# A row gradient streamed through three slots: where the third store is issued, and how loads and stores take turns on one DMA queue

## The chip, the cores and the metric

The kernel runs on one core of one Trainium2 chip. The metric is the device time of one execution in microseconds (us); the time before is the median of three runs, 1417.23 us, with 1416.08 and 1429.57 as the lowest and the highest. Engines are named as in the profile: DVE (VectorE), POOL (GpSimd) and SP (SyncE, which only issues DMAs here); SPq and POOLq are their instruction queues.

## The reference

```python
def setup_inputs():
    return {"x": np.random.randn(8192, 8192).astype(np.float32)}

def reference(x):
    return np.gradient(x, axis=1)
```

Along each row of 8192 numbers the result is `(x[j+1] - x[j-1]) / 2` inside, `x[1] - x[0]` in the first column and `x[8191] - x[8190]` in the last. So 268.44 MB are read from HBM and 268.44 MB are written, with one subtraction and one halving for each element.

## The kernel before, in words

The 8192 rows are cut into `nsets` = 32 tiles of 256 rows. A tile puts two whole rows into each of the 128 partitions, 64 KB a partition and 8.39 MB in all; in HBM a tile is one contiguous block. Tile `i` lives in slot `i % 3` of three buffers (`slots`, line 41). A slot has 64 spare elements ahead of the data, and the result is written in place, shifted down by these 64 elements, so one slot holds a tile from the start of its load to the end of its store.

For each tile the work is:

- the load (line 61, in `load`), one DMA on SP's queue. It may start when the store of tile `i - 3`, the last user of the slot, has landed (line 62).
- `ends` (line 71), a small subtraction on POOL: the four end values of the two rows a partition holds, taken before they are overwritten. It is the first instruction that waits for the load.
- the difference (line 82), one DVE instruction over 16,382 elements a partition, which subtracts the neighbours, halves, and writes in place. It waits for `ends`.
- the copy of the end values into the first and last columns (line 93), on POOL where `i % 5` is 1 or 3, else on DVE.
- the store. For `i % 3` of 0 and 1 it is one DMA on SP's queue (line 103). For `i % 3` = 2 it is two DMAs on POOL's own queue (line 99), each of 64 partitions, with the rows in HBM grouped as 8 groups of 8.

The last tile is computed and stored in two halves (`nr`, line 78).

The order on each queue is the order in which the program is written (`manual_schedule`, line 64). Three loads come first; then, after the store of every tile with `i % 3` = 2, the next three loads are issued together (lines 108 to 110). So SP's queue holds load, load, load, store, store, and again load, load, load, store, store. SP issues one DMA after another, and an instruction that waits for a semaphore holds back all those behind it. The function `chain` (line 46) names the waits that each instruction needs.

Of the kernel before, what the change touches and what calls it, by code (L numbers as in the profile page):

```python
# [1 line left out]

# [4 lines left out]


@with_exitstack
def kernel(  # L10
    ctx: ExitStack,
    tc: tile.TileContext,
    x: bass.AP,
    out: bass.AP,
):

    nc = tc.nc
    P = nc.NUM_PARTITIONS
    n, m = x.shape
    R = 2  # L30
    NB = 3
    SH = 64
    W = R * m
    nsets = n // (P * R)
    f32 = x.dtype

    x_sets = x.rearrange("(s p t) m -> s p (t m)", p=P, t=R)
    out_sets = out.rearrange("(s p t) m -> s p (t m)", p=P, t=R)

    pool = ctx.enter_context(tc.tile_pool(name="pool", bufs=1))  # L40
    slots = [pool.tile([P, SH + W], f32, name=f"slot{k}", tag=f"slot{k}") for k in range(NB)]
    ends = pool.tile([P, nsets, R, 2], f32, name="ends", tag="ends")
    loads, stores = [], [[] for _ in range(nsets)]
    in_front = {}

    def chain(i, ins, *needed):

        group, engine = f"slot{i % NB}", ins.ins.engine  # L50
        keep = [o.ins for o in needed]
        if in_front.get(engine, (None,))[0] == group:
            keep.append(in_front[engine][1])
        tc.declare_no_dep(ins.ins, group=group, keep=keep, reason="implied by the needed step")
        tc.add_to_no_dep_group(group, ins.ins)
        in_front[engine] = group, ins.ins
        return ins

    def load(i):
        b = slots[i % NB]  # L60
        ins = nc.sync.dma_start(out=b[:, SH : SH + W], in_=x_sets[i])  # L61
        loads.append(chain(i, ins, *(stores[i - NB] if i >= NB else [])))

    with tc.manual_schedule():
        for i in range(NB):
            load(i)
        for i in range(nsets):
            b = slots[i % NB]
            xin = b[:, SH : SH + W].rearrange("p (t m) -> p t m", m=m)

            ins = nc.gpsimd.tensor_sub(  # L71
                out=ends[:, i, :, :],
                in0=xin[:, :, 1 : m : m - 2],
                in1=xin[:, :, 0 : m - 1 : m - 2],
            )
            at = [chain(i, ins, loads[i])]
            last = i == nsets - 1
            nr = 1 if last else R
            for r in range(0, R, nr):
                c0, c1 = r * m + 1, (r + nr) * m - 1  # L80

                ins = nc.vector._custom_dve(  # L82
                    dve_ops.TENSOR_TENSOR_REDUCE_SUB_MAX,
                    out=b[:, c0:c1],
                    in0=b[:, SH + c0 + 1 : SH + c1 + 1],
                    in1=b[:, SH + c0 - 1 : SH + c1 - 1],
                    s0=0.0,
                    s1=0.5,
                )
                halved = chain(i, ins, *at)  # L90
                res = b[:, r * m : (r + nr) * m].rearrange("p (t m) -> p t m", m=m)
                placer = nc.gpsimd if i % 5 in (1, 3) and not last else nc.vector
                ins = placer.tensor_copy(out=res[:, :, 0 : m : m - 1], in_=ends[:, i, r : r + nr, :])  # L93
                placed = chain(i, ins, halved)
                if i % NB == NB - 1:

                    for h in range(2):
                        rows = out_sets[i, 64 * h : 64 * h + 64, :].rearrange("(a c) w -> a c w", a=8)
                        ins = nc.gpsimd.dma_start(out=rows, in_=b[64 * h : 64 * h + 64, 0:W])  # L99
                        stores[i].append(chain(i, ins, placed))  # L100
                    at = [halved]
                    continue
                ins = nc.sync.dma_start(
                    out=out_sets[i, :, r * m : (r + nr) * m], in_=b[:, r * m : (r + nr) * m]
                )
                stores[i].append(chain(i, ins, placed))
                at = [halved]
            if i % NB == NB - 1:
                for k in range(i + 1, min(i + 1 + NB, nsets)):
                    load(k)  # L110


# [1 line left out]
_INS = ['x']  # L114
_OUTS = [((8192, 8192), 'float32')]


# [23 lines left out]
```

## Time and profile before

| | |
|---|---|
| median of three runs | 1417.23 us (1416.08 to 1429.57) |
| the profiled execution's own time | 1416.08 us |
| its span, first to last instruction | 1414.2 us |
| DVE busy | 554.8 us, 39% of the span, 54 instructions |
| the difference, line 82, full tile | 31 instructions of 17.2 us |
| POOL busy | 19.8 us, 1% of the span |
| POOL's 20 store issues, line 99 | 11.0 us in all, 0.55 us each |
| SP's load issues, line 61 | 32, 0.34 us each (median) |
| SP's store issues, line 103 | 23, 0.34 us each (median) |
| HBM | 268.44 MB read, 268.44 MB written, 380 GB/s over the span |

How to read the profile: times are in us unless marked ns. A group of instructions is named by its line, engine and operation, and by the tensors it writes and reads (`slot<-in_x_dram` is a load, `out_dram<-slot` a store). The page of the profile has the busy share of each engine in 40 equal slices of the span, and under it the mean busy share of the 16 DMA engines and the GB/s that they moved. The queue numbered q1 is the one that SP's DMAs go through, q0 the one of POOL's. A share of the 16 engines is the time that a queue's packets took, divided by 16 times the span; where one DMA engine has packets of two queues under way, both are counted, so that a sum can pass 1. In the table of stretches, "DMA share" is the same for a stretch of time, and the last column is GB/s.

### The profile page before, as it was taken

Reading aid. Unit: us, or ns where it says so; the run is one execution under the profiler, and the core shown is the slowest. Engines: PE = TensorE matmul, PEld = TensorE weight load, DVE = VectorE, ACT = ScalarE, POOL = GpSimd, SP = SyncE. Lnnn points to the kernel's source line nnn. Section 1 sums busy time; section 2 is a strip of 40 time slices with the busy share of each in tenths; the row PEclk is TensorE's granted clock in tenths of the full one; section 3 lists DMA queues with packets and bytes.
Section 4 is the critical chain, followed back from the end, with each engine's and each line's share of the span. In section 5 each row is a group of like instructions: output and inputs, shape, how many; then the busy total and the mean of one; then the engine's idle time right before and its main releaser. Section 6 shows DMA issues by size and latency. Waiting matters only on the chain.

```text
span 1414.2 us, 269 instructions
## 1 busy us (share of the span) xinstructions
DVE 554.8 (39%) x54; POOL 19.8 (1%) x68
## 2 busy tenths in 40 slices
DVE  3820481048006700860094028304900950283063
POOL 0000000000000000000000000000000000000000
DMA  9999999999999999999999999999999999999959
GB/s 415 415 356 285 436 432 319 324 437 430 319 358 430 434 297 393 426 393 323 397 408 345 361 424 397 326 382 412 443 326 400 432 369 356 417 402 360 380 235 391
DMA packets 9522, 536.89 MB, mean 380 GB/s; under 512 B 1200, under 2 KB 1200, under 8 KB 1200
## 3 DMA queue, kind: packets, MB, share of 16 engines
q1 hardware_dynamic: 7920, 452.99, 76.9%
q0 software_dynamic: 1600, 83.89, 20.5%
q14 instruction: 2, 0.02, 0.0%
HBM read 268.44 MB, written 268.44 MB: 380 GB/s over the span
## 4 chain that ended last, share of the span: by engine, by line
another core or an unknown queue 47%; DMA 33%; DVE 15%; issue 3%; POOL 1%; SPq 0%; POOLq 0%
DMA slot<-in_x_dram 18%; DVE slot L82 15%; DMA out_dram<-slot 14%; POOL out_dram L99 0%; POOL ends L71 0%; SPq L61 0%; DVE slot L93 0%; POOL slot L93 0%; POOLq L136 0%; POOLq L99 0%
## 5 line engine op out<-in xcount | busy, mean ns | idle before, releaser
L82 DVE CUSTOM_DVE_ANT_0 slot<-slot 128x16382 f32<-128x16382 f32 (+1 forms) x33 | 551.3, 16706 | 837.0 <-POOL ends L71 837.0
L71 POOL TENSOR_TENSOR ends<-slot 128x4 f32<-128x4 f32 x32 | 6.3, 196 | 1039.1 <-DMA slot<-in_x_dram 1039.1
L99 POOL DMA_DIRECT2D out_dram<-slot x20 | 11.0, 553 | 107.8 <-DVE slot L93 106.6
L93 POOL COPY slot<-ends 128x4 f32<-128x4 f32 x12 | 2.3, 190 | 207.9 <-DVE slot L82 207.9
L93 DVE COPY slot<-ends 128x4 f32<-128x4 f32 (+1 forms) x21 | 3.6, 172 | 0.7
L125 POOL MEMSET const-float32-0.0<- 128x1 f32 x1 | 0.1, 98 | 0.2 <-issue 0.2
L125 POOL MEMSET const-bfloat16-1.0<- 128x1 bf16 x1 | 0.1, 101 | 0.0
L125 POOL MEMSET const-uint8-127<- 128x1 uint8 x1 | 0.1, 101 | 0.0
L125 POOL MEMSET const-float32-1.0<- 128x1 f32 x1 | 0.1, 98 | 0.0
## 6 DMA issues: line engine op xcount, KB each, us to landing
out_dram<-slot SPq DMA_DIRECT2D x2, 4096.0 KB, 20.2
slot<-in_x_dram SPq DMA_DIRECT2D x32, 52.2
out_dram<-slot SPq DMA_DIRECT2D x21, 41.5
out_dram<-slot POOLq DMA_DIRECT2D x20, 49.5
```

Source lines behind the costliest of these rows:

```text
L71: ins = nc.gpsimd.tensor_sub(out=ends[:, i, :, :], in0=xin[:, :, 1 : m : m - 2], in1=xin[:, :, 0 : m - 1 : m - 2],)
L82: ins = nc.vector._custom_dve(dve_ops.TENSOR_TENSOR_REDUCE_SUB_MAX, out=b[:, c0:c1], in0=b[:, SH + c0 + 1 : SH + c1 + 1], in1=b[:, SH + c0 ...
L93: ins = placer.tensor_copy(out=res[:, :, 0 : m : m - 1], in_=ends[:, i, r : r + nr, :])
L99: ins = nc.gpsimd.dma_start(out=rows, in_=b[64 * h : 64 * h + 64, 0:W])
L125: nc = _bacc.Bacc("TRN2", target_bir_lowering=False, num_devices=1)
```

## The change

The store of every tile goes through SP's queue as one DMA; POOL issues no DMA any more. The loads follow in pairs: after the store of each odd tile `i` come the loads of tiles `i + 2` and `i + 3`, in place of three loads after every third tile. SP's queue then holds load, load, load, store, store, load, load, store, store, load, load, and so on. The number of slots, the tiles, the computation, and the engine that places the end values of each tile stay as they were; DVE keeps its instructions in their order; SP's list grows by the 10 stores and POOL's loses its 20 halves. Lines move up in the changed kernel: the load is line 59, `ends` line 69, the difference line 80, the copy line 91 and the store line 93.

```diff
@@
-    loads, stores = [], [[] for _ in range(nsets)]
+    loads, stores = [], [None] * nsets
@@ def load(i):
         ins = nc.sync.dma_start(out=b[:, SH : SH + W], in_=x_sets[i])
-        loads.append(chain(i, ins, *(stores[i - NB] if i >= NB else [])))
+        loads.append(chain(i, ins, *([stores[i - NB]] if i >= NB else [])))
@@
                 placed = chain(i, ins, halved)
-                if i % NB == NB - 1:
-
-                    for h in range(2):
-                        rows = out_sets[i, 64 * h : 64 * h + 64, :].rearrange("(a c) w -> a c w", a=8)
-                        ins = nc.gpsimd.dma_start(out=rows, in_=b[64 * h : 64 * h + 64, 0:W])
-                        stores[i].append(chain(i, ins, placed))
-                    at = [halved]
-                    continue
                 ins = nc.sync.dma_start(
                     out=out_sets[i, :, r * m : (r + nr) * m], in_=b[:, r * m : (r + nr) * m]
                 )
-                stores[i].append(chain(i, ins, placed))
+                stores[i] = chain(i, ins, placed)
                 at = [halved]
-            if i % NB == NB - 1:
-                for k in range(i + 1, min(i + 1 + NB, nsets)):
+            if i % 2 == 1:
+                for k in range(i + 2, min(i + 4, nsets)):
                     load(k)
```

## The prediction

> **What bounds the kernel now.** I read the page first, then SP's waits, a table of stretches cut at POOL's stores, the timeline of one group of three tiles, and the start of the chain.
>
> ```profile
> span 1414.2 us, 269 instructions
> ...
> DVE  3820481048006700860094028304900950283063
> ...
> DMA  9999999999999999999999999999999999999959
> GB/s 415 415 356 285 436 432 319 324 437 430 319 358 430 434 297 393 426 393 323 397 408 345 361 424 397 326 382 412 443 326 400 432 369 356 417 402 360 380 235 391
> ...
> q1 hardware_dynamic: 7920, 452.99, 76.9%
> q0 software_dynamic: 1600, 83.89, 20.5%
> ```
>
> The 16 DMA engines are busy from end to end; DVE is not (39%). So the DMA engines are the bound. But equal busy shares do not move equal data: a slice moves 415 to 443 GB/s, or 285 to 330. Per queue: q1 moves 452.99 MB in 76.9% of 1414.2 us, 416.5 GB/s; q0, which is POOL's, 83.89 MB in 20.5%, 289 GB/s. The next view cuts the time at POOL's stores: from their issue until the third load behind them is issued (odd rows), and from there to the next (even rows).
>
> ```profile
> 80.60:146.50 65.90, 0.00 (x0) 1.18 (x2) 1.00 1.02 318
> 146.50:217.20 70.70, 52.01 (x5) 0.78 (x4) 1.00 0.99 430
> 217.30:286.30 69.00, 0.00 (x0) 1.06 (x2) 1.00 1.00 319
> 286.30:357.20 70.90, 51.84 (x4) 0.97 (x5) 1.00 1.00 433
> ...
> 826.20:897.00 70.80, 52.02 (x5) 0.78 (x4) 1.00 0.94 408
> ```
>
> The last two columns are the DMA share and GB/s. With POOL's store under way the engines are as busy (1.00 to 1.02) and move 318 or 319 GB/s; without it, 430 or 433. The nine even stretches give 408 to 433, about 424 weighted by length. DVE works in the even rows only, so it is not DVE that slows the transfers.
>
> ```profile
> 178.37 19.64 SPq L103 DMA_DIRECT2D out_dram<-slot  x2
> 179.98 0.20 POOL L71 TENSOR_TENSOR ends<-slot 128x4 f32<-128x4 f32 x1 [1.64 <-DMA slot<-in_x_dram]
> ...
> 199.31 0.20 POOL L71 TENSOR_TENSOR ends<-slot 128x4 f32<-128x4 f32 x1 [19.14 <-DMA slot<-in_x_dram]
> ...
> 217.27 1.09 POOL L99 DMA_DIRECT2D out_dram<-slot  x2 [17.76 <-DVE slot L93]
> 218.60 67.73 SPq L61 DMA_DIRECT2D slot<-in_x_dram  x3
> ```
>
> This is the clock of the transfers. The second load of this group lands at 179.98 and the third at 199.31: 19.33 us for 8.39 MB, 434 GB/s. A store issued at 178.37 stands behind that load; the load that waits for it goes out at 218.60, 19.29 us after 199.31. So a store takes what a load does, and passing from loads to stores cost nothing here. Then the three loads take SP 67.73 us to issue, since each waits for a store and the third for both POOL halves.
>
> ```profile
> 0.74 21.93 DMA slot<-in_x_dram
> ```
>
> The first load, on an empty queue, takes 21.93 us from issue to landing. So 2.6 us (21.93 - 19.33) are start and landing together: a DMA issued 2.6 us or more before the one ahead of it lands leaves no gap.
>
> **The loss in time.** POOL's stores are issued at 80.55, 217.27, 357.22 and so on to 1284.73: 133.8 us from one to the next. A group is six transfers, 6 x 19.33 = 116.0. So 17.8 us a group are lost, 160.2 over nine groups. From 1286.04, when the last two loads go out, six transfers are left: 1286.04 + 116.0 + 1.0 (last landing to end of span) = 1403.0, against 1414.2: 11.2 more. Without these 171.4 us the span would be 1242.8. From the other side: 22.67 (first landing) + 63 x 19.33 + 1.0 = 1241.5. The two agree; I take 1242.
>
> **The change part by part.**
>
> *POOL's stores go to SP's queue* (20 DMAs out, 10 in). The ten tiles' transfers then cost 19.33 each as the others do, and the packets of two queues no longer meet on the engines. That is the whole gain, -171 to -173.
>
> *POOL loses 20 issues of 0.55 us,* 11.0 us in all: nothing, POOL is busy 1%. *SP gains 10 issues of 0.34 us,* 3.4 us: nothing while a transfer stands in the queue, 3.4 at most.
>
> *The order of SP's queue.* Here a wait could come in, because SP stops at each load. Let T = 19.33 and let the store of tile i-1 (i odd) start at 0. It lands at T, and the load of tile i+2, which waited for it, is issued; the queue still has the store of i, T of work against the 2.6 it needs: 16.7 to spare. The store of i lands at 2T, and the load of i+3 is issued, again with 16.7 to spare. Behind it SP was holding the store of i+1, long computed: issued at 2T, needed at 4T, no delay. The load of i+2 lands at 3T; `ends`, the difference and the copy take 17.7 (first tile: 22.74 to the store's issue at 40.43), so the store of i+2 is issued at 3T + 17.7 and needed at 5T: 38.7 - 17.7 - 2.6 = 18.4 to spare. The next load waits for the store of i+1, which lands at 5T. No link is late, for every pair; DVE needs 35 us of 77.3. The covers are the transfer ahead in the queue. If they were gone, each pair would pay up to 17.7 + 2.6 = 20.3.
>
> ```profile
> SPq L61 <- DMA out_dram<-slot: 809.0, 29, 54.0
> ```
>
> These waits remain, of about one T in place of up to 54.0, and stay hidden for the same reason. At the end the store of tile 30 no longer stands behind a late load, and the two halves of tile 31 (8.7 us of DVE each) are ready before the store of 30 is through: cost nothing.
>
> *From stores to loads, 15 times.* Before, a load behind a store on q1 always had POOL's store beside it, so the price of this passage is not shown clean. Lower end 0: loads to stores at 199.31 cost 0. Upper end by the largest excess of a transfer without POOL's: the third load lands at 62.58, 20.53 after the second at 42.05, 1.2 too much; 15 x 1.2 = 18. I take 0.3 each, near the rows without excess (the same pair of loads is 19.31 to 19.34 in the later groups I read): 5. A gain is excluded, as no transfer took less than 19.3.
>
> **Sum.** 1242 + 5 = 1247 of span; the profiled execution's own time is 1416.08 for 1414.2, so +1.9: **1249**. The median of the runs shown is 1.15 above the profiled one.
>
> [...]
>
> **The rivals.**
>
> *Not POOL's queue but the passage from stores to loads is what is slow (slower).* For: each slow stretch begins just where loads follow stores, and what is left when POOL's store is gone is not shown. Against: q1's packets move 416.5 GB/s by their own share and q0's 289, and the slow stretch lasts some 65 us, while a passage is a moment. Price: 17.8 each, 15 of them in place of ten groups: 1244 + 267 = 1511. It decides from (1416 - 1244) / 15 = 11.5 us a passage.
>
> *The queue runs dry part of the way (faster, less).* An engine that is ahead of the slowest by over 16.7 us has nothing to do until the landing is complete. For: near the end of before the engines are out of step; slices of one us there show one tenth busy:
>
> ```profile
> DMA  9999799999967313031130311311011109109090
> ```
>
> (1340 to 1380 us). Against: this follows POOL's stores, and the changed kernel has only one form of transfer, with equal shares. Price: 5 us a pair gives 1249 + 75 = 1324; 2 to 10 give 1279 to 1399.
>
> *No change.* The engines' busy share is already 97% and the bytes are the same; if mixing reads and writes set the 380 GB/s, the time stays 1416. Against: the even stretches hold loads and stores too.
>
> **How the numbers follow.** Forecast 0.74, with a range of its own of 1242 to 1272: below, no cost at the passages; above, all data at the 424 GB/s of the even stretches (536.89 MB / 424 = 1266, + 4.3 for start and end, + 1.9). Partly dry 0.12, no change 0.04, slower 0.10. All data at q1's 416.5 would give 1295; a range of 1240 to 1300 holds the forecast and the near half of the second case, 0.80. A change under 1% is about what a measurement here cannot tell from none: faster 0.86, same 0.04, slower 0.10.
>
> **What would show it.** Right: q0 gone from the table of queues, slices of 425 to 435 GB/s throughout, loads landing 19.3 apart in pairs and pairs 77.3 apart, one store wait of about 19 us before each load. Wrong: a low slice in each pair (passage), tenths under 9 in the DMA line (dry), or a load landing more than 20.5 after the one before with the queue full.

## The result, and the profile after

| | before | after |
|---|---|---|
| median of four runs each, us | 1419.72 (1416.08 to 1429.57) | 1248.37 (1248.06 to 1249.45) |
| ratio, with its 95% interval | | 0.8785 (0.8738 to 0.8832) |
| profiled execution, and its span, us | 1416.08, 1414.2 | 1248.15, 1246.1 |

The change takes 171 us off. The forecast was 1249 with a span of 1247. Here and below, medians and ranges are over all runs of a kernel, and ratios over its runs within 1.5% of the fastest, against runs of the kernel before that were taken with them. The page of the changed kernel, with the same lines as were shown of before:

```profile
span 1246.1 us, 240 instructions
...
DVE  2851905519055190551905519064290642806423
...
DMA  9999999999999999999999999999999999999998
GB/s 404 438 438 429 414 435 438 438 438 433 433 429 431 429 433 435 435 438 431 433 438 427 425 438 438 438 429 435 431 438 435 429 427 433 435 433 435 435 438 362
...
q1 hardware_dynamic: 9360, 536.88, 99.7%
```

The DMA line was nines in all slices but one before, and is again: it could not tell the two kernels apart. The GB/s line does. No slice between the first and the last is under 414, where before it fell every few slices, down to 285 and near the end to 235. The bound is the same, the 16 DMA engines (97.4% before, both queues together, and 99.7%); what they move is not (380 GB/s over the span before, 431 after).

The timeline of the changed kernel from the first pair on (`ends` at line 69 is the first to see a load land; line 59 are the loads, line 93 the stores):

```profile
81.73 20.05 SPq L59 DMA_DIRECT2D slot<-in_x_dram  x2
101.82 36.71 SPq L93 DMA_DIRECT2D out_dram<-slot  x2
120.45 0.20 POOL L69 TENSOR_TENSOR ends<-slot 128x4 f32<-128x4 f32 x1 [57.85 <-DMA slot<-in_x_dram]
...
140.00 0.20 POOL L69 TENSOR_TENSOR ends<-slot 128x4 f32<-128x4 f32 x1 [1.84 <-DMA slot<-in_x_dram]
...
159.38 19.82 SPq L59 DMA_DIRECT2D slot<-in_x_dram  x2
...
198.04 0.20 POOL L69 TENSOR_TENSOR ends<-slot 128x4 f32<-128x4 f32 x1 [57.84 <-DMA slot<-in_x_dram]
```

In this pair the loads land 19.55 apart, and the next pair follows 77.59 later (120.45 to 198.04); four transfers at 19.33 are 77.32. Over the whole span the pairs follow each other every 77.58 on average. The two stores behind a pair go out within 36.71 us, one at once and one when its tile is computed, well inside the 77. And SP's own waits:

```profile
SPq L59 <- DMA out_dram<-slot: 577.8, 29, 21.6
```

29 loads wait for a store, 577.8 us in all, 19.9 each; before it was 809.0, with one of 54.0. The waits have become even, not short, and they are hidden: a transfer always stands ahead in the queue, and no slice between the ends falls under 414 GB/s.

### The profile page after: what moved, and what is told of

The parts are those of the page before. It is cut to its first block, busy times and chain, and to the rows that moved or that the text cites. A ratio compares the mean times of both kernels' runs of the same rounds, so it can differ in the third digit from the quotient of the medians.

```text
span 1246.1 us, 240 instructions
## 1 busy us (share of the span) xinstructions
DVE 554.8 (45%) x54; POOL 8.9 (1%) x48
## 3 DMA queue, kind: packets, MB, share of 16 engines
q1 hardware_dynamic: 9360, 536.88, 99.7%
## 4 chain that ended last, share of the span: by engine, by line
DMA 52%; DVE 21%; another core or an unknown queue 20%; issue 5%; SPq 0%; POOL 0%; POOLq 0%
DMA slot<-in_x_dram 45%; DVE slot L80 21%; DMA out_dram<-slot 7%; SPq L93 0%; POOL ends L69 0%; DVE slot L91 0%; POOL slot L91 0%; POOLq L126 0%; SPq L59 0%
```

## The experiments

The sum had come out, but it rested on a reading that had not been tested: that POOL's store was slow because the packets of two queues met on the engines. That theory (the queue) stood against the form of the store (two halves of 64 partitions, grouped by 8), and both against the order of loads and stores (the passage). Each edit below is against the kernel before, unless it says otherwise. "Third store" is that of the tiles with `i % 3` = 2.

### Without the pairs: three and three on SP

This takes away POOL's queue and the halves together, as the change does, and keeps the order by threes.

```diff
-                if i % NB == NB - 1:
-                    for h in range(2):
...
-                    continue
                 ins = nc.sync.dma_start(
```

> Only the queue of the third store is changed: it goes through SP's queue as one DMA, and the order stays three loads, then three stores. The theory that the second queue or the form of its store was the loss (both call for it) expects 64 transfers of 19.33 us and 10 passages from stores to loads at the 0.25 us that the changed kernel shows a pair: 1245 to 1250. The rival that the order by pairs brings part of the gain expects a time above 1265, with low slices where three loads wait for three stores.

1248.03 us (1247.75 to 1248.18), ratio 0.8767 (0.8709 to 0.8825). The whole gain is there without the pairs. In the same place of the timeline three loads now go out in 39.33 us, where before they took 58.1 to 67.7:

```profile
81.61 39.33 SPq L61 DMA_DIRECT2D slot<-in_x_dram  x3
139.76 0.20 POOL L71 TENSOR_TENSOR ends<-slot 128x4 f32<-128x4 f32 x1 [77.24 <-DMA slot<-in_x_dram]
```

The order by pairs brings nothing of its own.

### The order alone: pairs, with POOL's halves kept

This is the changed kernel with the block of lines 95 to 102 of before put back.

```diff
+                if i % NB == NB - 1:
+                    for h in range(2):
...
+                    continue
                 ins = nc.sync.dma_start(
```

> Only the order is changed: loads by pairs as in the changed kernel, but every third store stays on POOL's queue in two halves. The theory that the loss belongs to POOL's store expects ten times some 17 us above 1248, so 1390 to 1430, and low slices of about 320 GB/s wherever q0 is at work. The rival that the order brings part of the gain expects 1250 to 1370.

1489.72 us (1483.76 to 1501.59), ratio 1.0451 (1.0362 to 1.0541): above both expectations, and slower than before. SP's waits and a stretch of it show why:

```profile
SPq L59 <- DMA out_dram<-slot: 979.7, 24, 101.7
```

```profile
240.00:297.00 57.00, 17.22 (x1) 0.38 (x2) 1.00 1.00 278
```

The queues in the last 17 us of that stretch, from 280 to 297 us:

```profile
q0 software_dynamic: 51, 3.15, 83.5%
q1 hardware_dynamic: 29, 0.85, 14.6%
```

A load that waits for a store stands at the head of SP's queue for up to 101.7 us (54.0 before), and a store that is ready stands behind it: one whose tile was done at 258.87 goes out at 301.93. At the end of that wait q1 has little to offer (14.6%), and the engines move POOL's slow store nearly alone: 4.00 MB of both queues in these 17 us, 235 GB/s. So POOL's halves are slow even where few packets of q1 run beside them. The pairs are harmless with all stores on the one queue and costly beside POOL's halves; pairs beside a whole store on POOL were not run.

### The form: POOL's store in one piece

```diff
-                    for h in range(2):
-                        rows = out_sets[i, 64 * h : 64 * h + 64, :].rearrange("(a c) w -> a c w", a=8)
-                        ins = nc.gpsimd.dma_start(out=rows, in_=b[64 * h : 64 * h + 64, 0:W])
-                        stores[i].append(chain(i, ins, placed))
+                    ins = nc.gpsimd.dma_start(out=out_sets[i], in_=b[:, 0:W])
+                    stores[i].append(chain(i, ins, placed))
```

> The kernel before, with POOL's store as one DMA of 128 partitions in place of two halves of 64 grouped by 8; it stays on POOL's queue. If two queues on the same engines are the cause (queue theory), the time stays at 1390 to 1430 and q0's packets remain slow. If the form of the store is the cause (form theory), the time falls to 1250 to 1270 with 425 to 435 GB/s while both queues are at work.

1266.2 us (1252.66 to 1285.33), ratio 0.8819 (0.8726 to 0.8912). The two fastest of the four runs took 1252.66 and 1258.11. With the second queue still in use, nearly all of the gain is there. From 80 to 125 us, while POOL's store and SP's loads run side by side:

```profile
DMA packets 352, 19.92 MB, mean 443 GB/s; under 512 B 48, under 2 KB 48, under 8 KB 48
...
q1 hardware_dynamic: 208, 11.53, 59.2%
q0 software_dynamic: 144, 8.39, 43.0%
```

A share divided by the megabytes is the price of a byte: 59.2 / 11.53 = 5.13 for q1 and 43.0 / 8.39 = 5.13 for q0. A byte costs the same on both, and together they move 443 GB/s. In the page of before the same division gives 76.9 / 452.99 = 0.170 and 20.5 / 83.89 = 0.244. It was not the queue that made q0's bytes dear. The queue theory falls as the main cause; what is left of it is the distance of this kernel from 1248, 4 to 10 us in the two fastest runs.

### The form without the second queue: the halves on SP

```diff
-                        ins = nc.gpsimd.dma_start(out=rows, in_=b[64 * h : 64 * h + 64, 0:W])
+                        ins = nc.sync.dma_start(out=rows, in_=b[64 * h : 64 * h + 64, 0:W])
```

> The kernel before, with the two halves of 64 partitions grouped by 8 issued on SP's queue in place of POOL's: the form without the second queue. Queue theory: 1245 to 1255. Form theory: each of the 20 halves uses only some of the 16 engines; if both halves fall on the same eight, each group has eight engines idle for up to 19.3 us, 1249 + 10 x 19.3 = 1442; if they spread over all, but with slow packets, 1350 to 1420.

1450.94 us (1433.69 to 1499.5, ten runs), ratio 1.0130 (1.0074 to 1.0187). The form alone carries all of the loss; the 1.3% beyond it are a small difference. Stretches of the first group in the profiled run, one of 1464.48 us: ahead of the halves, then in the first half:

```profile
85.00:95.00 10.00, 0.00 (x0) 0.00 (x0) 1.00 0.97 419
...
108.00:118.00 10.00, 0.00 (x0) 0.00 (x0) 1.00 1.03 210
```

The loads that wait for the last store ahead of the halves, and for the halves:

```profile
101.17 38.64 SPq L61 DMA_DIRECT2D slot<-in_x_dram  x2
```

All 16 engines are busy (a mean share of 1.03), at 210 GB/s, half of the 419. The first of the two loads goes out at 101.17, when the last store ahead of the halves has landed, and the second, whose issue of 0.33 ends that 38.64, at 139.5, when both halves have. So the third store takes some 38.3 us, twice 19.3. The expected 1442 is near the time, but it had eight engines idle, and by the share of 1.03 none is: the packets are slow on all. On POOL's queue the same halves cost 1.3% less in sum. That q1's transfers run beside them there is the likely reason; it was not tried by itself.

### Grouping, or halves?

Four edits took the form apart, all with the third store on SP's queue. In the first two it is one DMA of 128 partitions, its HBM rows grouped as 16 groups of 8, and as 8 groups of 16:

```diff
-                    for h in range(2):
-                        rows = out_sets[i, 64 * h : 64 * h + 64, :].rearrange("(a c) w -> a c w", a=8)
-                        ins = nc.gpsimd.dma_start(out=rows, in_=b[64 * h : 64 * h + 64, 0:W])
+                    rows = out_sets[i].rearrange("(a c) w -> a c w", a=16)
+                    ins = nc.sync.dma_start(out=rows, in_=b[:, 0:W])
```

> [...] The rival that the split into halves of 64 partitions, each on some of the engines, is the cause: 1246 to 1255.

1247.99 us (1247.1 to 1248.14), ratio 0.8770 (0.8714 to 0.8825). The grouping as the cause had been put at 1400 to 1470.

> [...]

1247.89 us in a single run, where the grouping as the cause had been put at up to 1441, or at 1550 to 1870. These ranges were the author's estimates; how the groups are shared out among the engines is in no trace. Both expectations built on the grouping fell: with all 128 partitions in the DMA, the grouping costs nothing, in either form (1248.03 without it, in three and three). The third has the halves without the grouping:

```diff
-                        rows = out_sets[i, 64 * h : 64 * h + 64, :].rearrange("(a c) w -> a c w", a=8)
-                        ins = nc.gpsimd.dma_start(out=rows, in_=b[64 * h : 64 * h + 64, 0:W])
+                        rows = out_sets[i, 64 * h : 64 * h + 64, :]
+                        ins = nc.sync.dma_start(out=rows, in_=b[64 * h : 64 * h + 64, 0:W])
```

> The kernel before, with the two halves of 64 partitions on SP's queue without the grouping by 8. [...] The rival that only the grouping counts (runs of 8 neighbours, or 512 KB runs in HBM for each engine): 1246 to 1260.

1451.3 us, in the 1400 to 1470 at which the halves as the cause had been put; its four runs lie between 1421.13 and 1488.32, too far apart for a ratio, and all far above 1248. The stretch in the first half, in the run of 1488.32 us, reads as that of the halves by 8:

```profile
108.00:118.00 10.00, 0.00 (x0) 0.00 (x0) 1.00 1.03 210
```

From 128 to 136 us, in the second half, it is 213 GB/s. So it is the halves. Two readings are left: a DMA of 64 partitions is slow wherever they lie (size), or the lower or the upper 64 are (place).

### Size or place?

Even and odd partitions in place of the lower and upper half:

```diff
-                        rows = out_sets[i, 64 * h : 64 * h + 64, :].rearrange("(a c) w -> a c w", a=8)
-                        ins = nc.gpsimd.dma_start(out=rows, in_=b[64 * h : 64 * h + 64, 0:W])
+                        ins = nc.sync.dma_start(out=out_sets[i, h:P:2, :], in_=b[h:P:2, 0:W])
```

> The kernel before, with the third store on SP's queue in two DMAs of 64 partitions, but even and odd partitions in place of the lower and the upper half. The halves moved some 210 GB/s, 5.1 us a packet on all 16 engines. [...] Size theory (a DMA of 64 partitions is slow wherever they lie): 1420 to 1490.

1247.14 us (1246.87 to 1248.1), ratio 0.8777 (0.8723 to 0.8831); place had been put at 1248 to 1260. The same place of the timeline, through both DMAs and into the load behind them:

```profile
101.00:110.00 9.00, 0.00 (x0) 0.00 (x0) 1.00 0.94 408
110.00:118.00 8.00, 0.00 (x0) 0.00 (x0) 1.00 1.06 459
118.00:128.00 10.00, 0.00 (x0) 0.00 (x0) 1.00 0.97 419
```

Two DMAs of 64 partitions, and nothing lost. Then the middle 64 partitions first, and the outer quarters after them:

```diff
-                    for h in range(2):
-                        rows = out_sets[i, 64 * h : 64 * h + 64, :].rearrange("(a c) w -> a c w", a=8)
-                        ins = nc.gpsimd.dma_start(out=rows, in_=b[64 * h : 64 * h + 64, 0:W])
+                    for p0, p1 in ((32, 96), (0, 32), (96, 128)):
+                        ins = nc.sync.dma_start(out=out_sets[i, p0:p1, :], in_=b[p0:p1, 0:W])
```

> The kernel before, with the third store on SP's queue in three DMAs: partitions 32 to 95, then 0 to 31, then 96 to 127. Place theory: the middle 64 lie half in the lower and half in the upper half, so 16 engines do not meet and it takes 9.7 us; each of the other two is in one half and takes 2 x 5.1 = 10.2: 30.1 in place of 38.6, so ten times 10.8 above 1248, 1340 to 1375. Size theory: the middle one takes 20.4 as the halves did, and the sum is that of the halves or more: 1420 to 1490.

1346.32 us (1344.29 to 1382.08), ratio 0.9471 (0.9377 to 0.9565). In the middle DMA, and in the outer ones:

```profile
101.00:110.00 9.00, 0.00 (x0) 0.00 (x0) 1.00 0.96 401
...
118.00:128.00 10.00, 0.00 (x0) 0.00 (x0) 1.00 1.06 262
```

Within one store the rate falls as the partitions change: 401 GB/s for the 64 that straddle the middle, 262 in a stretch of the outer ones, in whose last microsecond the next load begins. 1346 - 1248 = 98, for 108 expected. Size falls; place stands.

The 210 GB/s of the halves, the 408 to 459 of the alternate partitions, the 401 of the middle 64 and the 262 of the outer quarters all agree with place. Why the lower or the upper half alone is slow, and whether engines meet there, the runs do not show.

### A second queue of SP's kind

```diff
-                    for h in range(2):
-                        rows = out_sets[i, 64 * h : 64 * h + 64, :].rearrange("(a c) w -> a c w", a=8)
-                        ins = nc.gpsimd.dma_start(out=rows, in_=b[64 * h : 64 * h + 64, 0:W])
+                    ins = nc.scalar.dma_start(out=out_sets[i], in_=b[:, 0:W])
```

> The kernel before, with the third store as one DMA of 128 partitions on ACT's queue: a second queue, but one of the same kind as SP's. With the whole store on POOL's queue four runs gave 1252.66 to 1285.33, some of them above the 1248 of the single queue. If any second queue costs that, through engines that get out of step, the time here is 1250 to 1290 too and varies as much; if it comes from POOL's queue alone, 1247 to 1252 in all runs.

1253.28 us (1248.47 to 1258.06), ratio 0.8808 (0.8747 to 0.8869). The lowest run fits the second expectation and the other three the first, so the run decides little: a second queue costs from nothing to some 10 us on ACT, and 4 to 10 on POOL in the two fastest runs. Neither gains anything, and the single queue repeats to about 0.1%. In its page a byte costs the same on both queues (84.2 / 452.99 and 15.5 / 83.89, 0.186 and 0.185):

```profile
q1 hardware_dynamic: 7920, 452.99, 84.2%
q10 hardware_dynamic: 1440, 83.89, 15.5%
```

Where those few us go, and why they differ from run to run, stays open.

### The price of a passage, and of a dry queue

Two edits of the changed kernel. One load after each store from tile 1 on, one transfer always ahead:

```diff
-            if i % 2 == 1:
-                for k in range(i + 2, min(i + 4, nsets)):
-                    load(k)
+            if 1 <= i and i + 2 < nsets:
+                load(i + 2)
```

> The changed kernel with one load after the store of each tile from tile 1 on (of tile i+2, which waits for the store of i-1): 29 passages from stores to loads in place of 15, and one transfer always ahead in the queue. My own theory (a passage costs about 0.25 us, the queue never runs dry): 1248 + 14 x 0.25 = 1252, 1247 to 1256. Passage rival: at the 1.2 us of the dearest transfer seen, 1265, and above that if reading and writing in turn costs more.

1251.44 us (1249.85 to 1252.25), ratio to before 0.8805 (0.8751 to 0.8859). 14 more passages cost 3.1 us, about 0.2 each (0.22 from the medians). And the load that waits for the very store just issued:

```diff
-            if i % 2 == 1:
-                for k in range(i + 2, min(i + 4, nsets)):
-                    load(k)
+            if i + NB < nsets:
+                load(i + NB)
```

> The changed kernel with one load after the store of each tile, of tile i+3, which waits for that very store, the last thing in the queue: the cover is taken away. My own theory of the dry queue: each of 29 loads then starts on an empty queue and pays the 2.6 us between a landing and the next transfer's first data and landing, with nothing else lost as the next store is already computed: 1248 + 29 x 2.6 = 1323, 1310 to 1340. A rival that in-order waiting costs more (the stores behind each load come late too, up to 20.3 us each): 1400 to 1840. That a dry queue costs nothing: 1248.

1356.66 us (1355.23 to 1357.5), ratio to before 0.9546 (0.9487 to 0.9605). The queue is dry before each of the 29 loads, and that costs 108 us, 3.7 a load in place of the 2.6 expected:

```profile
81.68 0.33 SPq L59 DMA_DIRECT2D slot<-in_x_dram  x1
82.05 0.43 SPq L93 DMA_DIRECT2D out_dram<-slot  x1
104.97 0.20 POOL L69 TENSOR_TENSOR ends<-slot 128x4 f32<-128x4 f32 x1 [42.41 <-DMA slot<-in_x_dram]
...
124.24 0.33 SPq L59 DMA_DIRECT2D slot<-in_x_dram  x1
```

From the load's issue to its landing are 23.2 us (81.68 to 104.9), where the very first load of before, with two more loads behind it, took 21.93; the store behind it lands 19.3 later. So 1.3 of the 3.7 come with a store behind the load. That is about the 1.2 by which the third load of the first group was late in before, with a store behind it too. Why this passage is dear after a fresh start and cheap in the flow was not tried. The mechanism was as expected, without the larger prices of the rival.

## Why the prediction was right, and where its reason was wrong

**The loss, 171 us.** Right in size: 1419.72 - 1248.37 = 171.4, and the sum said 171 to 173 for the span. It came from counting transfers against a clock of 19.33 us read off the timeline, and that count does not depend on the cause: the change took away the second queue and the form at once. That was luck. Moving the halves to SP's queue as they were takes the second queue away too, and by the same reason would have come to the 1245 to 1255 of the queue theory; it took 1451.

**The cause.** Wrong. The step that failed reads "The ten tiles' transfers then cost 19.33 each as the others do, and the packets of two queues no longer meet on the engines. That is the whole gain, -171 to -173." The first half of it holds. But packets of two queues met without loss in the whole store on POOL (443 GB/s) and on ACT. What was taken away was the split into the lower and the upper 64 partitions, 38.3 us a store in place of 19.3 on SP's own queue too. The reading of "416.5 GB/s" against "289 GB/s" as a property of the queues was the slip: q0 differed from q1 in the queue and in the form at once, and nothing in that profile parts the two. It did speak against the meeting of packets, though. From 101 to 131 us of before both queues moved the same:

```profile
q0 software_dynamic: 79, 4.13, 63.4%
q1 hardware_dynamic: 79, 4.19, 36.3%
```

At 19.33 us for 8.39 MB, 4.19 MB take 32% of these 30 us. So the loads cost little more than at that rate (36.3 against 32), and POOL's halves beside them twice as much (63.4). Packets that slow each other by meeting should be dear on both queues.

For whole stores the runs find no gain from a second queue, and a small price: 1248 on one queue, 1248 to 1258 on two (the four runs on ACT, the two fastest on POOL).

**No link in SP's order is late.** Right: no slice is low and the loads' waits are even at 19.9 us. The cover is real: taken away, it cost 3.7 us a load. The 2.6 used for it was too low by 1.1, which the 16.7 to spare hid. The 20.3 a pair, named as the most that a lost cover could cost, was not reached: two loads paid 7.5.

**0.3 us a passage.** Right in size: 0.26 a pair on average over the span, 0.22 by the run with 14 more of them. Not in place: the second load of a pair lands 19.59 after the first on average over the 14 full pairs, and the other three transfers take 57.99, three times 19.33. So all of the 0.26 falls on the load that has a store behind it, which the forecast had at nothing, and none where a load follows a store.

**Issues of POOL and SP at nothing.** Nothing shows against it.

**One reading was too clean.** The page's slices do not move either 415 to 443 or 285 to 330 GB/s: 18 of the 40 lie between these groups. The stretches with POOL's store under way move 318 to 361, not 318 or 319 throughout. The sum did not use either.

**The rivals.** The passage as the cause fell twice: three and three, with the ten passages of before, runs at 1248, and a passage costs 0.22. That nothing would change fell with the 171 us. No dry stretch appeared. The engines out of step near the end of before went with the halves, as the argument against that rival had it: the last slice but one moves 235 GB/s before, 246 with the halves on SP's queue, 402 in three and three.

**A faster version?** None. The single queue, in threes or in pairs, and the alternate halves all stand at 1247 to 1248; 64 x 19.33 = 1237 of that are transfers at 434 GB/s.

## What to carry to other kernels

A busy share of 97% on the DMA engines does not say that they move what they can (380 GB/s here, and 431 at 99.7%): divide bytes by share, by queue and by stretch, and time one transfer with nothing beside it. Where a slow transfer differs from the others in two ways, the profile cannot say which one it is; one run for each way can. Cut a store along its columns (the last tile's two halves here: from its load's landing to the end of the span two tiles' stores took 39.5 us, 2 x 19.33 and 0.9) or by alternate partitions (1247 us here) rather than into the lower and the upper half (1451), and keep one whole transfer ahead of any that has to wait (108 us here without it).

## What the runs showed of the hardware that was not expected

- A store of partitions 0 to 63 or 64 to 127 runs at 210 and 213 GB/s with all 16 engines counted busy (shares of 1.03 and 1.00), one of even or odd partitions at 408 to 459.
- Grouping the HBM rows of a contiguous store of 128 partitions, as 16 groups of 8 or 8 of 16, changes nothing: 1247.99 and 1247.89 us, and 1248.03 without it.
- Two queues share the engines without loss of rate (443 GB/s), yet the time with two varies more, 1248.5 to 1258.1 on ACT, than with one, 1248.1 to 1249.5 in the changed kernel.
- A load that finds the queue dry, with a store behind it, costs 3.7 us more than one behind another transfer, not 2.6.
